# Two slack terms in a planned order, small passes on all partitions, and where the compressed scores run, in a two-layer hybrid decoder

## The chip, the cores and the metric

The kernel runs on one core of one Trainium2 chip. A core has four compute engines that each take their instructions in order: TensorE (PE in the profile), which multiplies matrices and transposes; VectorE (DVE); ScalarE (ACT); and GpSimd (POOL), which is all but unused here. SyncE (SP) issues the DMA transfers between the chip's main memory and the on-chip memory. The engines run side by side and wait for each other through semaphores only. PE's results land in PSUM, eight banks of 128 partitions by 512 float32 values; everything else lies in SBUF, also 128 partitions wide.

The metric is the device time of one execution in microseconds, the median of several runs.

## The reference

Two layers (`DEPTH` = 2) over a sequence of 256 positions with 1024 features. Each layer has two groups of attention heads side by side and a feed-forward part, each wrapped in RMS norms. All of it is float32.

```python
h = _rms_norm(x, g_pre_mix[l])
nq, kc, vc, ksel, vsel, kwin, vwin, gates, fq, fk, fv, ff = jnp.split(h @ w_in[l], split_at, axis=-1)
o_nsa = _nsa_mixer(...)        # 8 heads, 2 groups of keys and values
o_fox = _fox_mixer(...)        # 8 heads
mix = jnp.concatenate([o_nsa, o_fox], axis=-1) @ w_out[l]
x = x + _rms_norm(mix, g_post_mix[l])
h = _rms_norm(x, g_pre_mlp[l])
y = jnp.square(jax.nn.relu(h @ w_up[l])) @ w_down[l]
x = x + _rms_norm(y, g_post_mlp[l])
```

The sparse attention (`_nsa_mixer`) sums three branches under sigmoid gates. The compressed branch makes 15 blocks of 32 positions out of the keys and the values, sends each through a small network with a GELU (`gelu(blocks @ w1 + b1) @ w2 + b2`), and attends to the results:

```python
kc = _compress(k_c, pos_k, w1_k, b1_k, w2_k, b2_k)
vc = _compress(v_c, pos_v, w1_v, b1_v, w2_v, b2_v)
sc = jnp.einsum('bghqd,bgnd->bghqn', qp, kc) * scale
pc = _masked_softmax(sc, mc) * mc
o_cmp = jnp.einsum('bghqn,bgnd->bghqd', pc, vc)
```

The selected and the windowed branch attend to whole keys; at 256 positions both are plain causal attention with their own keys and values. The forgetting attention (`_fox_mixer`) adds differences of a running sum to its logits:

```python
log_f = jax.nn.log_sigmoid(f_logits + f_bias)
cum = jnp.cumsum(log_f, axis=1).transpose(0, 2, 1)
logits = einsum('bhqd,bhkd->bhqk', q, k) * scale + cum[:, :, q0:q1, None] - cum[:, :, None, :q1]
```

## The kernel before, in words

**Weights.** All weights come from main memory in pieces of 288 to 512 KB, in the order in which PE needs them (`Weights`, lines 465 to 500). A large float32 product is made of three products of half the width: each operand is split into `hi`, rounded to the type `fp32r`, and `lo`, the rounded rest; hi·hi, hi·lo and lo·hi are summed in PSUM (`mm3`, line 651). For a piece of weights ACT makes `whi` (a copy that rounds) and DVE makes `wlo` (a subtraction). The buffers are rings (`raw` of 9, `whi` and `wlo` of 7).

**Stages of a layer.** The input projection has six chunks of columns, c0 to c5. c0 and c1 hold the keys and values of the sparse part, the gates and the forget logits, c2 its queries, c3, c4 and c5 the queries (`fqT`), keys (`fkT`) and values (`fV`) of the forgetting part. The weights of the compressed branch's small network ride along with the pieces of c2 and c3 (`SEQ`, `RIDES`, `hidden_part`, line 884): at the fourth piece of c2 the 16 products for the keys run, at the fourth piece of c3 those for the values. They use only 32 columns of PE each, four of them side by side (`tile_position=(0, 32 * c)`; `kstk` and `kstv` are the stationary operands). Then follow, on other engines' help, `hidden_T` (line 899) and `hidden_gelu` (919) for the GELU, `compressed_k` (927), which leaves the keys as `kbd`, a block-diagonal tile for two heads, and `compressed_v` (937), which leaves the values split into halves in `vrep`; `compressed_vT` (953) transposes that into `vbig`. `compressed_scores` (964) is the four products `kbd` by `qT`, again on 32 columns each, `compressed_exp` (973), `compressed_scale` (985) and `compressed_T` (1001) are its softmax and transposes. `forget_sums` (1012) makes the running sum by a product with a triangle of ones and leaves `cum`: rounded values on partitions 0 to 31 and 64 to 95, the rounded rests on 32 to 63 and 96 to 127.

Attention itself goes over 24 entries of a list `flat` (line 1308): 16 for the sparse part (pair of heads, parity, branch) and 8 for the forgetting part ("fox"). For each there are scores (`nsa_scores` or `fox_scores`, in the score banks `s` and `x`), a masked maximum on DVE and an exponential on ACT (`pr`, with `st` for maxima and sums), the scaling by sum and gate on DVE (`scale`, line 1193), the transposes (`probs_T`, 1204: the products named `s<-cst,pr`), which ACT or DVE copies to `prT` or `prX`, and for each two pairs of heads a run of values' products (`pv`, 1222, in the bank `o`) on 64 columns each. `o_evac` (1240) splits the result into `oT` hi (ACT) and `oT` lo (DVE), which the output projection multiplies (the products `acc<-whi,oT` and so on). The `sandwich` (704) applies the norms; the MLP (lines 1392 to 1499) follows.

**Order.** Nothing is issued as it is written. A `Recorder` (line 171) records every operation with what it depends on. `stretch` (186) makes several PE products one unit; this is how the runs of small products stay together. `fill`, `fill_to` and `step` pull products of the projection's chunks between the steps of the attention, and a dictionary `side` (1310) names what else is called at which entry of `flat`; from there on an operation's key grows by `LANE` = 0.9 for each recorded operation. Each operation gets a planned cost in ns (`_cost`, 439, with `_latency` and `_product`). `schedule` (290) then plays all engines: at each moment each engine takes, of the operations that are ready and whose buffers fit, the one of lowest rank. For PE the rank is the key; for the others, from the second pass on, it is the time by which the operation must end so that PE's users in the pass before would not be late (`deadlines`, 247). A change of PE's tile size is charged with `ENTER` and `LEAVE` (line 367). `order` (275) makes one pass and `PASSES` = 4 further ones and keeps the one with the least planned end. `emit` (390) issues that order; so nearly all instructions stand at line 397 in the trace, and the names of tiles tell them apart. The planned times set the order only; on the chip each engine starts an instruction when its semaphores allow.

A load's planned end is when the bus is through with it, and 2900 ns (line 364).

Of the kernel before, what the change touches and what calls it, by code (L numbers as in the profile page):

```python
# [24 lines left out]
P = 128  # L25
# [11 lines left out]
LANDING = 2500.0  # L37
WAIT = 0.7
# [17 lines left out]
C_ID, C_ROPE, C_SID, C_TRI, C_MASK, C_CM, C_M01, C_SEL, C_END = np.cumsum(  # L56
    [0, 128, 64, 32, 256, 256, 32, 32, 16]).tolist()


def constants():  # L60
    c = np.zeros((P, C_END), np.float32)
    i = np.arange(P)
    c[:, C_ID:C_ID + P] = np.eye(P)
    causal = np.where(i[None, :] <= i[:, None], 0.0, NEG)
    c[:, C_MASK + 128:C_MASK + 256] = causal
    c[:, C_TRI:C_TRI + 128] = i[:, None] <= i[None, :]
    c[:, C_TRI + 128:C_TRI + 256] = 1.0
    inv = np.float32(500000.0) ** (-np.arange(8, dtype=np.float32) * np.float32(2.0) / np.float32(16.0))
    for t in range(NT):
        ang = (i + t * P).astype(np.float32)[:, None] * inv[None, :].astype(np.float32)  # L70
        o = C_ROPE + 32 * t
        c[:, o:o + 8] = c[:, o + 8:o + 16] = np.cos(ang)
        c[:, o + 16:o + 24] = -np.sin(ang)
        c[:, o + 24:o + 32] = np.sin(ang)
        ok = (16 * np.arange(16) + 31)[None, :] <= (i + t * P)[:, None]
        c[:, C_CM + 16 * t:C_CM + 16 * t + 16] = np.where(ok, 0.0, NEG)
        c[:, C_M01 + 16 * t:C_M01 + 16 * t + 16] = ok
    for h in range(8):
        c[h::32, C_SEL + h] = 1.0
    for m in range(32):  # L80
        c[m::32, C_SID + m] = 1.0
    return c
# [88 lines left out]
class Recorder:  # L171
# [21 lines left out]
    def add(self, engine, name, args, kw):  # L193
# [15 lines left out]
        op.cost = _cost(op, views)  # L209
# [80 lines left out]
    def schedule(self):  # L290
# [41 lines left out]
        while events:  # L332
# [5 lines left out]
            for e, ops in waiting.items():  # L338
                while busy[e] <= t:
# [21 lines left out]
                    if e == "sync":  # L361
                        busy[e] = t + 450
                        bus = max(bus, t + 1150) + best.cost
                        best.end = bus + 2900
                    else:
                        busy[e] = best.end = t + best.cost
                        if e == "tensor" and best.tile != tiled:
                            busy[e] = best.end = best.end + (tiled == (P, P)) * ENTER + (tiled != (P, P)) * LEAVE
                            tiled = best.tile
# [69 lines left out]
def _cost(op, views):  # L439

    out = op.args[0] if op.args else op.kw["out"]
    n = int(np.prod(out.shape[1:]))
    if op.engine == "sync":
        v = views[0][1]
        return v.shape[0] * int(np.prod(v.shape[1:])) * 4 / 360.0
# [5 lines left out]
    if op.engine == "vector":  # L451
# [7 lines left out]
        return 68 + 64 * aps + n * (0.52 if fast else 1.04) + 10 * (op.name == "tensor_tensor_reduce")  # L459
# [55 lines left out]
def trunk(nc, A, consts_in, out, sbp, pp):  # L515
    def tile(shape, dtype, name, tag=None, bufs=1):
        return nc.tile(sbp[(tag or name) not in OPERANDS], shape, dtype, name, tag, bufs)
# [108 lines left out]
    nc.vector.memset(kbd, 0.0)  # L626
    vrep = tile([P, 2, 4, 2, 16], F32R, name="vrep")
    nc.vector.memset(vrep.bitcast(F32), 0.0)
# [149 lines left out]
    for l in range(DEPTH):  # L778
# [105 lines left out]
        def hidden_part(s, q):  # L884
# [3 lines left out]
            if q == 3:  # L888
                T["hid"] = psum("o")
                with nc.stretch():  # L890
                    for i in range(16):
# [3 lines left out]
                                         start=i < 4, stop=i >= 12, tile_position=(0, 32 * c))  # L895
                T["hs" + s] = tile([P, 256], F32, name="hs", tag="cum")
# [29 lines left out]

        def compressed_k():
# [4 lines left out]
            for j in range(2):  # L932
                hh = slice(j * HD, j * HD + HD)
                nc.vector.tensor_scalar(kbd[hh, :, j, :], ps[hh, 0:32].rearrange("p (g n) -> p g n", g=2),
                                        par["smT"][hh, 36:37], None, op0=OP.add)

        def compressed_v():
# [3 lines left out]
            for c in range(2):  # L941
                nc.tensor.matmul(ps[:, 0:32], par["w2"]["v"][:, c].rearrange("p j d -> p (j d)"), T["ghv"][:, c, :],
                                 start=c == 0, stop=c == 1)
            vt = small([P, 2, 16], "vt", 1)
            nc.vector.tensor_scalar(vt, ps[:, 0:32].rearrange("p (g n) -> p g n", g=2), par["smT"][:, 37:38], None,
                                    op0=OP.add)
            for j in range(2):
                hh = slice(j * HD, j * HD + HD)
                x = vt[hh, :, None, :].to_broadcast([HD, 2, 2, 16])
                nc.vector.tensor_copy(vrep[hh, :, 0:2, j, :], x)  # L950
                nc.vector.tensor_sub(vrep[hh, :, 2:4, j, :], x, vrep[hh, :, 0:2, j, :].bitcast(F32))
# [12 lines left out]
        def compressed_scores():  # L964
            ps = psum("s")
            with nc.stretch():
              for p in range(4):
                nc.tensor.matmul(ps[32 * p:32 * p + 32, :S], kbd[:, p // 2].rearrange("p j n -> p (j n)"),
                                 T["qT"][:, p, :], start=True, stop=True, tile_position=(0, 32 * p))
            T["csT"] = small([P, S], "cs", 1)  # L970
            nc.scalar.activation(T["csT"], ps[:, :S], AF.Copy)

        def compressed_exp():
            ps = psum("s")
# [37 lines left out]
        def forget_sums():  # L1012
# [6 lines left out]
            cum = tile([P, 384], F32R, name="cum", tag="cum")  # L1019
            for o, n in ((0, P), (P, S)):  # L1020
                nc.scalar.activation(cum[:, o:o + n], ps[:, :n], AF.Copy)
            for r in (slice(32, 64), slice(96, 128)):
                for o, n in ((0, P), (P, S)):
                    nc.vector.tensor_sub(cum[r, o:o + n], ps[r, :n], cum[r, o:o + n].bitcast(F32))
# [277 lines left out]
        for t in range(NT):  # L1302
# [7 lines left out]
        side = {0: compressed_scores, 1: compressed_exp, 2: compressed_scale, 3: compressed_T,  # L1310
                4: lambda: (fill_to("c3"), hidden_T("v")), 5: lambda: hidden_gelu("v"),
# [236 lines left out]
```

## Time and profile before

| | |
|---|---|
| median of 3 runs | 627.24 us (627.1 to 627.25) |
| the profiled execution, its own time | 627.13 us |
| its span, from the first to the last instruction | 625.3 us |
| granted TensorE clock, mean | 0.998 |
| HBM traffic | 114.00 MB read, 1.05 MB written, 184 GB/s over the span |
| largest group of instructions on DVE | `wlo`, 188 passes, 225.4 us |
| largest group on ACT | `whi`, 188 passes, 195.2 us |
| largest group on PE | `s<-xT,whi`, 448 products of 512 columns, 112.0 us |

How to read it: the profile is one execution, taken by the hardware profiler. The span is what the trace covers; the 1.8 us between it and the execution's own time lie outside the trace. An instruction's line in a view gives the line of the kernel (here that of `emit`), the engine, the operation, the tile written and the tiles read, their sizes, and a count where equal neighbours are drawn together. PE's products are pipelined: their busy times overlap, so that the distance between two starts, not the busy time, is what a product costs. "PEld" is PE's loading of stationary operands, which overlaps with products. A name in brackets behind an instruction, such as [0.19 <-DVE vrep L397], is the time for which the engine waited ahead of it and what ended the wait.

In the page's 40 slices of the span PE is at nine tenths or more in all but the last. DVE is at eight or nine tenths from 16 to 125 us and again from 313 to 406 us, the attention of the two layers, and mostly at five to seven in the MLPs.

### The profile page before, as it was taken

How to read it: one execution, taken by the hardware profiler on the slowest of the kernel's cores; microseconds unless marked ns; L12 is line 12 of the kernel's file. 1: busy time of each engine (PE TensorE's matmuls, PEld its weight loads, DVE VectorE, ACT ScalarE, POOL GpSimd, SP SyncE). 2: the span in 40 equal slices, each digit the busy share in tenths (PEclk: the TensorE clock that was granted, in tenths of full speed). 3: DMA queues.
4: the chain of work that ended last, by engine and by line, in shares of the span. 5: the costliest groups of instructions: out<-in, count | busy, mean ns of one | idle time of the engine just before them, and what ended most of it. 6: DMA issues, size and time to landing. Idle time of an engine off the chain costs nothing.

```text
span 625.3 us, 9919 instructions
## 1 busy us (share of the span) xinstructions
PE 616.8 (99%) x3572; PEld 517.7 (83%) x3572; DVE 477.9 (76%) x1053; ACT 375.8 (60%) x728; POOL 0.2 (0%) x4
## 2 busy tenths in 40 slices
PE   9999999999999999999999999999999999999995
PEld 7988977788888888888888988777888888888884
DVE  6889998879966566567698899976996666566544
ACT  7768776567655455555476766764766555455432
POOL 0000000000000000000000000000000000000000
PEclk9999999999999999999999999999999999999999
DMA  8988555319666666654348682622386556666001
GB/s 324 404 310 285 199 161 157 91 64 320 221 200 202 187 183 203 193 178 128 117 129 273 231 313 67 226 85 95 123 306 187 191 179 198 197 179 202 24 1 67
DMA packets 33600, 115.69 MB, mean 185 GB/s; under 512 B 3984, under 2 KB 4112, under 8 KB 33552
## 3 DMA queue, kind: packets, MB, share of 16 engines
q1 hardware_dynamic: 33552, 115.07, 56.5%
q8 instruction: 28, 0.46, 0.3%
q14 instruction: 20, 0.16, 0.1%
HBM read 114.00 MB, written 1.05 MB: 184 GB/s over the span
## 4 chain that ended last, share of the span: by engine, by line
PE 87%; DVE 10%; issue 1%; DMA 1%; ACT 0%; DVEq 0%; SPq 0%
PE s L397 33%; PE acc L397 25%; PE x L397 24%; PE o L397 6%; DVE wlo L397 3%; DVE pr L397 3%; DMA first<-in_first_dram 1%; DVE gz L397 1%; DVE cs L397 0%; DVE fqT L397 0%; DVE prT L397 0%; DVE st L397 0%; DVE prX L397 0%; ACT whi L397 0%; DVE vrep L397 0%
## 5 line engine op out<-in xcount | busy, mean ns | idle before, releaser
L397 DVE TENSOR_TENSOR wlo<-wraw,whi 128x1024 fp32r<-128x1024 f32 (+1 forms) x188 | 225.4, 1203 | 85.1 <-ACT whi L397 81.9
L397 ACT ACTIVATE whi<-wraw 128x1024 fp32r<-128x1024 f32 (+1 forms) x188 | 195.2, 1042 | 111.8 <-PE acc L397 64.6
L397 PE MATMUL s<-xT,whi 128*128 128x512 f32 x448 | 112.0, 392 | 0.0
L397 PEld LDWEIGHTS s<-xT,whi 128*128 128x128 f32 x448 | 81.4, 189 | 15.2
L397 PE MATMUL acc<-whi,aT 128*128 128x512 f32 x256 | 88.6, 390 | 0.0
L397 PE MATMUL x<-whi,aT 128*128 128x512 f32 x256 | 88.4, 390 | 0.0
L397 PEld LDWEIGHTS s<-xT,wlo 128*128 128x128 f32 x448 | 61.1, 190 | 4.4
L397 PE MATMUL s<-xT,wlo 128*128 128x256 f32 x448 | 62.5, 282 | 0.0
L397 ACT ACTIVATE pr<-pr,st 128x256 f32<-128x256 f32 (+1 forms) x96 | 43.2, 452 | 24.8 <-DVE st L397 21.9
L397 PEld LDWEIGHTS acc<-whi,aT 128*128 128x128 f32 x256 | 48.1, 188 | 9.9
L397 PEld LDWEIGHTS x<-whi,aT 128*128 128x128 f32 x256 | 48.1, 188 | 9.7
L397 PE MATMUL acc<-wlo,aT 128*128 128x512 f32 x128 | 50.0, 390 | 0.0
L397 PE MATMUL x<-wlo,aT 128*128 128x512 f32 x128 | 50.0, 390 | 0.0
L397 PE MATMUL acc<-xT,whi 128*128 128x256 f32 x256 | 49.8, 286 | 0.0
L397 PEld LDWEIGHTS acc<-xT,whi 128*128 128x128 f32 x256 | 40.6, 190 | 1.6 <-ACT whi L397 0.4
L397 ACT ACTIVATE rl<-h 128x512 f32<-128x512 f32 x28 | 17.7, 633 | 35.8 <-DVE h L397 35.8
L397 PE MATMUL x<-whi,xT 128*128 128x512 f32 x112 | 37.1, 403 | 0.1
L397 PE MATMUL acc<-xT,wlo 128*128 128x256 f32 x128 | 36.4, 284 | 0.0
L397 PE MATMUL acc<-whi,xT 128*128 128x512 f32 (+1 forms) x128 | 36.3, 356 | 0.0
L397 DVE TENSOR_TENSOR h<-rl 128x512 f32<-128x512 f32 x28 | 19.4, 692 | 16.8 <-ACT rl L397 16.8
L397 ACT ACTIVATE rl<-x 128x512 f32<-128x512 f32 x24 | 14.8, 617 | 24.5 <-PE x L397 18.7
L397 PEld LDWEIGHTS acc<-wlo,aT 128*128 128x128 f32 x128 | 24.0, 188 | 4.9
(222 smaller groups left out, 975.4 us busy)
## 6 DMA issues: line engine op xcount, KB each, us to landing
wraw<-in_w_up_dram SPq DMA_DIRECT2D x64, 512.0 KB, 3.7
wraw<-in_w_down_dram SPq DMA_DIRECT2D x64, 512.0 KB, 3.5
wraw<-in_w_in_dram SPq DMA_DIRECT2D x36, 512.0 KB, 4.9
wraw<-in_w_out_dram SPq DMA_DIRECT2D x16, 512.0 KB, 5.6
w<-in_cmp_w_k_dram SPq DMA_DIRECT2D x8, 512.0 KB, 6.0
w<-in_cmp_w_v_dram SPq DMA_DIRECT2D x8, 512.0 KB, 5.8
first<-in_first_dram SPq DMA_DIRECT2D x7, 384.0 KB, 6.0
wraw<-in_w_in_dram SPq DMA_DIRECT2D x8, 288.0 KB, 4.3
```

Of the source, the lines that this page charges most:

```text
L397: getattr(getattr(self.nc, op.engine), name)(*[real(v) for v in args], **{k: real(v) for k, v in kw.items()})
```

## The change

Four things are changed.

The planner's costs: each DVE and ACT operation costs 20 ns more in the plan (`SLACK`), and a DVE operation that writes fewer than 128 partitions 100 ns more (`part`). A load's landing is the same 2900 ns, written as 900 + `LATE`.

Passes on parts of the partitions become passes on all: `kbd` and the compressed values `vt` are now made by `by_half`, for each group of keys one pass over all 128 partitions that multiplies by a constant which is one on the half of the partitions that belongs to the head and zero on the other (`C_HALF`). With the zeros written each time, the two memsets at the kernel's start go. `vrep` hi is one pass on ACT and `vrep` lo one on DVE, in place of two and two passes on DVE over 64 partitions each. `forget_sums` has two ACT copies into a new tile `two` (its ring is that of `rl`): `hi`, and the sum times `C_REST`, which is one on the partitions of the rests and zero elsewhere; two passes on DVE over all partitions then form `cum`, in place of two ACT copies and four DVE subtractions on 32 partitions each.

The compressed scores: the four products `kbd` by `qT` stand in the stretch of the values' 16 products in `hidden_part`, behind them; their copy out of PSUM is the first step of `compressed_exp`.

The places of the steps: `side` now calls `fill_to("c3")` at entry 0 (which brings the values' products with it), `compressed_exp` at 1, `compressed_scale` and `hidden_T("v")` at 2, `compressed_T` and `hidden_gelu("v")` at 3; `compressed_v` at 6 and all behind it stay.

```diff
+SLACK, LATE = {"vector": 20, "scalar": 20}, 2000
...
-C_ID, C_ROPE, C_SID, C_TRI, C_MASK, C_CM, C_M01, C_SEL, C_END = np.cumsum(
-    [0, 128, 64, 32, 256, 256, 32, 32, 16]).tolist()
+C_ID, C_ROPE, C_SID, C_TRI, C_MASK, C_CM, C_M01, C_SEL, C_HALF, C_REST, C_END = np.cumsum(
+    [0, 128, 64, 32, 256, 256, 32, 32, 8, 2, 2]).tolist()
...
+    for j in range(2):
+        c[j * HD:j * HD + HD, C_HALF + j] = 1.0
+
+    c[:, C_REST] = i // 32 % 2
+    c[:, C_REST + 1] = 1 - i // 32 % 2 * 2
...
-        op.cost = _cost(op, views)
+        op.cost = _cost(op, views) + SLACK.get(engine, 0)
...
-                        best.end = bus + 2900
+                        best.end = bus + 900 + LATE
...
+    part = 100 * (out.shape[0] < P)
...
-        return 68 + 64 * aps + n * (0.52 if fast else 1.04) + 10 * (op.name == "tensor_tensor_reduce")
+        return 68 + part + 64 * aps + n * (0.52 if fast else 1.04) + 10 * (op.name == "tensor_tensor_reduce")
...
-    nc.vector.memset(kbd, 0.0)
...
-    nc.vector.memset(vrep.bitcast(F32), 0.0)
...
+                    if s == "v":
+                        compressed_scores()
...
+        def by_half(dst, ps, bias):
+
+            for g in range(2):
+                nc.vector.scalar_tensor_tensor(dst[:, g], ps[:, None, 16 * g:16 * g + 16].to_broadcast([P, 2, 16]),
+                                               par["smT"][:, bias:bias + 1],
+                                               cst[:, C_HALF:C_HALF + 2, None].to_broadcast([P, 2, 16]), op0=OP.add, op1=OP.mult)
+
...
-            for j in range(2):
-                hh = slice(j * HD, j * HD + HD)
-                nc.vector.tensor_scalar(kbd[hh, :, j, :], ps[hh, 0:32].rearrange("p (g n) -> p g n", g=2),
-                                        par["smT"][hh, 36:37], None, op0=OP.add)
+            by_half(kbd, ps, 36)
...
-            vt = small([P, 2, 16], "vt", 1)
-            nc.vector.tensor_scalar(vt, ps[:, 0:32].rearrange("p (g n) -> p g n", g=2), par["smT"][:, 37:38], None,
-                                    op0=OP.add)
-            for j in range(2):
-                hh = slice(j * HD, j * HD + HD)
-                x = vt[hh, :, None, :].to_broadcast([HD, 2, 2, 16])
-                nc.vector.tensor_copy(vrep[hh, :, 0:2, j, :], x)
-                nc.vector.tensor_sub(vrep[hh, :, 2:4, j, :], x, vrep[hh, :, 0:2, j, :].bitcast(F32))
+            vt = small([P, 2, 2, 16], "vt", 1)
+            by_half(vt, ps, 37)
+            x = vt.rearrange("p g j n -> p g (j n)")[:, :, None, :].to_broadcast([P, 2, 2, 32])
+            hi, lo = (vrep[:, :, b:b + 2].rearrange("p g a j n -> p g a (j n)") for b in (0, 2))
+            nc.scalar.activation(hi, x, AF.Copy)
+            nc.vector.tensor_sub(lo, x, hi.bitcast(F32))
...
-            ps = psum("s")
-            with nc.stretch():
-              for p in range(4):
+            T["cps"] = ps = psum("s")
+            for p in range(4):
                 nc.tensor.matmul(ps[32 * p:32 * p + 32, :S], kbd[:, p // 2].rearrange("p j n -> p (j n)"),
                                  T["qT"][:, p, :], start=True, stop=True, tile_position=(0, 32 * p))
+
+        def compressed_exp():
             T["csT"] = small([P, S], "cs", 1)
-            nc.scalar.activation(T["csT"], ps[:, :S], AF.Copy)
-
-        def compressed_exp():
+            nc.scalar.activation(T["csT"], T["cps"][:, :S], AF.Copy)
...
+            two = tile([P, 2, S], F32R, name="two", tag="rl", bufs=2)
+            hi, rest = two[:, 0], two[:, 1].bitcast(F32)
+            nc.scalar.activation(hi, ps[:, :S], AF.Copy)
+            nc.scalar.activation(rest, ps[:, :S], AF.Copy, scale=cst[:, C_REST:C_REST + 1])
             for o, n in ((0, P), (P, S)):
-                nc.scalar.activation(cum[:, o:o + n], ps[:, :n], AF.Copy)
-            for r in (slice(32, 64), slice(96, 128)):
-                for o, n in ((0, P), (P, S)):
-                    nc.vector.tensor_sub(cum[r, o:o + n], ps[r, :n], cum[r, o:o + n].bitcast(F32))
+                nc.vector.scalar_tensor_tensor(cum[:, o:o + n], hi[:, :n].bitcast(F32), cst[:, C_REST + 1:C_REST + 2],
+                                               rest[:, :n], op0=OP.mult, op1=OP.add)
...
-        side = {0: compressed_scores, 1: compressed_exp, 2: compressed_scale, 3: compressed_T,
-                4: lambda: (fill_to("c3"), hidden_T("v")), 5: lambda: hidden_gelu("v"),
+        side = {0: lambda: fill_to("c3"), 1: compressed_exp, 2: lambda: (compressed_scale(), hidden_T("v")),
+                3: lambda: (compressed_T(), hidden_gelu("v")),
                 6: compressed_v, 7: compressed_vT, 8: forget_sums, 14: lambda: fill_to("c4"), 17: lambda: fill_to("c5")}
```

The program has as many PE products after the change as before. The order on all engines is made anew by the planner; the prediction goes by the two orders as they come out of it.

## The prediction

> **What bounds the kernel now.** I read the page first, then the busy time by stage, then the chain of work that ended last, then TensorE's (PE) timeline at the places that the change touches.
>
> ```profile
> span 625.3 us, 9919 instructions
> PE 616.8 (99%) x3572; PEld 517.7 (83%) x3572; DVE 477.9 (76%) x1053; ACT 375.8 (60%) x728; POOL 0.2 (0%) x4
> PE 87%; DVE 10%; issue 1%; DMA 1%; ACT 0%; DVEq 0%; SPq 0%
> ```
>
> PE is busy 616.8 of 625.3 us, so hardly a gap can be closed. But a busy PE may still be a late one, and 10% of the chain lies on VectorE (DVE). The stages tell where (columns: stretch, its length, then busy us and count of PE, PE's weight loads, DVE, ACT, POOL; clock, DMA share, GB/s):
>
> ```profile
> 60.00:76.00 16.00, 15.81 (x129) 15.20 (x128) 15.85 (x65) 11.58 (x31) 0.00 (x0) 1.00 0.69 248
> 92.00:112.00 20.00, 20.00 (x137) 14.54 (x136) 17.96 (x63) 13.88 (x39) 0.00 (x0) 1.00 0.53 157
> 145.00:300.00 155.00, 155.00 (x791) 132.49 (x790) 107.74 (x131) 86.44 (x123) 0.00 (x0) 1.00 0.64 201
> ```
>
> In the sparse attention of a layer (60 to 76 us) PE and DVE are both full. In the later part (92 to 112) DVE has 2.0 us free of 20. In the MLP (145 to 300) PE is alone. The chain between 44 and 80 us (start, us, what):
>
> ```profile
> 48.16 1.23 DVE wlo L397
> ...
> 57.18 0.60 DVE fqT L397
> ...
> 69.40 0.32 DVE pr L397
> ...
> 70.99 1.12 DVE wlo L397
> ...
> 72.81 0.57 DVE prX L397
> ...
> 73.65 0.23 DVE vrep L397
> ...
> 74.02 0.93 PE s L397 x7
> ```
>
> From 48 to 74 us the chain runs along DVE and is handed to PE at `vrep`; from there to the end it stays on PE. So two things can be gained: PE work itself, and the few moments at which PE is late behind DVE. Both are small.
>
> **The change, part by part.** Sums are made against the profiled execution's 627.13 us: 625.3 of span and 1.8 around it; the median of the runs is 0.1 higher.
>
> *1. The compressed scores join the run of small tiles.* Both ways of running `tile_position=(0, 32 * c)` products stand in the trace, alone:
>
> ```profile
> 35.75 0.39 PE L397 MATMUL x<-whi,xT 128*128 128x512 f32 x1
> 36.07 1.93 PE L397 MATMUL o<-w,kstk 128*32 128x256 f32 x32
> 37.94 0.50 PE L397 MATMUL acc<-xT,whi 128*128 128x256 f32 x2
> 38.27 0.28 PE L397 MATMUL acc<-xT,wlo 128*128 128x256 f32 x1
> ...
> 53.12 0.39 PE L397 MATMUL x<-kx,qS 128*128 128x512 f32 x1
> 53.45 0.64 PE L397 MATMUL s<-qT,kbd 128*32 128x256 f32 x8
> 54.02 0.50 PE L397 MATMUL acc<-xT,whi 128*128 128x256 f32 x2
> 54.36 0.28 PE L397 MATMUL acc<-xT,wlo 128*128 128x256 f32 x1
> ```
> ```profile
> 613.35 5.45 PE acc L397 x24
> ```
>
> A plain product of 512 columns takes 5.45/24 = 0.23 us from start to start, one of 256 columns 0.12. The first run therefore occupies PE from 35.75 + 0.23 = 35.98 to 37.94, and the pair behind it takes 0.33 instead of 0.24: 2.05 us for 32 passes. The scores: 53.35 to 54.02, and 0.10 behind: 0.77 for 8 passes. Four groups of 8 and one group differ by 1.28, so a group is 0.43 and what a visit costs besides is 0.34. The scores keep their group and lose the visit, once a layer: 2 x 0.34 = **0.68 us less**. No row shows two different products in one run; if the visit's cost stays, the gain is 0. I take the whole, since the row of 32 shows four groups with other weights in one visit.
>
> [...]
>
> What the run now waits for: its last four products need `kbd`, and `kbd` stands in DVE's queue behind both `fqT` passes; all of PE is queued behind it. In layer 0, from the last product of c3's first half on, PE has 16 products of 256 columns, one of 512 and four groups of the run ahead: 16 x 0.12 + 0.23 + 4 x 0.43 = 3.9 us. DVE needs 2 x 0.60 and two small passes (part 3, 0.25 each), 1.7, and 0.1 to 0.2 for the handoff at either end: about 2.0. That leaves 1.9 us of cover, more than one `wlo` pass of 1.12. Cost: nothing; with the cover gone, what DVE is late, up to 1 us a layer.
>
> *2. The order.* The cost of every DVE and ACT instruction is raised by 20, of those on part of the partitions by 100 more, so the planner puts PE's users of their results later. PE's work is the same: 3,344 matmuls in both; the 859 of the first MLP and the last 871 stand in the same order. In the attention PE's visits to smaller tiles fall from 22 to 18: two by part 1, two because fox scores and the values' products now follow each other directly. That saves between 0 and a whole visit each; I take half of 0.34, as each place has three changes of mode instead of four: 2 x 0.17 = **0.34 less**.
>
> Where PE is late now (what precedes in the rows is the start, the busy time, the count):
>
> ```profile
> 73.43 0.40 PE L397 MATMUL acc<-xT,whi 128*128 128x256 f32 x2
> 74.02 0.33 PE L397 MATMUL s<-identr,vrep 128*128 128x128 f32 x2 [0.19 <-DVE vrep L397]
> ...
> 83.37 1.29 PE L397 MATMUL s<-cst,pr 128*128 128x128 f32 x6
> ```
> ```profile
> 380.98 0.28 PE L397 MATMUL acc<-xT,whi 128*128 128x256 f32 x1
> 381.43 0.34 PE L397 MATMUL s<-identr,vrep 128*128 128x128 f32 x2 [0.16 <-DVE vrep L397]
> ...
> 389.67 0.87 PE L397 MATMUL s<-cst,pr 128*128 128x128 f32 x6
> ...
> 391.32 0.39 PE L397 MATMUL acc<-wlo,xT 128*128 128x512 f32 x1
> 392.04 0.50 PE L397 MATMUL s<-kx,qS 128*128 128x256 f32 x2 [0.34 <-DVE st L397]
> ```
>
> At `vrep` PE is 0.59 - 0.24 = 0.35 late in layer 0 and 0.45 - 0.12 = 0.33 in layer 1. In the new order 14 products of 512 columns (9 `whi`, 5 `wlo`) stand ahead of the first `vrep` transposes that stood behind before: 14 x 0.23 = 3.2 us more cover; 9 in layer 1, 2.0 us. DVE's queue ahead of the same point gains one `wlo` (1.12) and two `fkT` (as `fqT`, 0.60 each), loses one `prX` (0.57) and one pair of `pr` scalings (0.32 and a bit less): 1.2 more. So 2.0 and 0.8 us of lead are won, against 0.35 and 0.33 of lateness. I take both waits as gone: **0.68 less** (bounds 0 and 0.68).
>
> The six `pr` transposes at 83.37 take 0.42 longer than the same six at 389.67; at 391.32 PE stands 0.72 - 0.23 = 0.49. With these two and some three smaller ones of 0.1 to 0.2 I count 1.3 us of other lateness. Summed over both orders in such durations, PE's 48 rounds of `pr` transposes come later against DVE's scalings in 39 cases, by up to 7 us, and earlier in 9, by at most 1.6; there the trace has at least 1.8 us between scaling and transposes. So the old waits should mostly go; but the order is new everywhere, and I take half: **0.66 less** (bounds 0 and 1.3).
>
> What gets tighter is the way out of the values' products:
>
> ```profile
> 119.68 0.50 PE L397 MATMUL acc<-whi,oT 128*128 128x512 f32 x1
> ```
> ```profile
> 119.80 0.60 ACT L397 ACTIVATE oT<-o 128x512 fp32r<-128x512 f32 x1 [1.83 <-PE o L397]
> ```
> ```profile
> 120.43 0.69 DVE L397 TENSOR_TENSOR oT<-o,oT 128x512 fp32r<-128x512 f32 x1 [0.43 <-ACT oT L397]
> ```
>
> From 119.68, PE's first product after the run, `oT`'s upper part is ready at 120.40 (0.72) and its lower part at 121.12 (1.44). Before, 12 products stand between the last fox run and the first that needs its `oT`; now 4 (0.9 us), and 7 for the lower part (1.6). Behind the second sparse run there were 19, now six transposes alone (0.63 to 0.67 by 389.67 and its like) in layer 0 and three products more in layer 1. By the rows this is just enough for fox and 0.05 to 0.2 short for the sparse one. At the start, the loads of `x` and the chains of `rsqrt` for both row blocks now go ahead of the third piece of c1's weights; I allow 0.2 for it. New waits in all: **0.4 more** (bounds 0 and 1.7, four handoffs each a bit late).
>
> *3. All partitions.* Off PE's path; it thins DVE's queue:
>
> ```profile
> L397 DVE TENSOR_SCALAR kbd<-s,w 64x32 f32<-64x32 f32 x4 | 1.0, 247 | 0.0
> L397 DVE TENSOR_TENSOR vrep<-vt,vrep 64x64 fp32r<-64x64 f32 x4 | 0.9, 220 | 0.1
> L397 DVE CAST vrep<-vt 64x64 fp32r<-64x64 f32 x4 | 0.8, 191 | 0.1
> ...
> L397 DVE TENSOR_TENSOR cum<-s,cum x8: 283/356/429, 78.7 to 386.3; 32x256 fp32r<-32x256 f32 x4, 32x128 fp32r<-32x128 f32 x4
> ...
> L397 DVE SCALAR_TENSOR_TENSOR z<-acc,rsqrt,bias 128x32 f32<-128x32 f32 x4 | 1.0, 243 | 0.0
> L397 DVE SCALAR_TENSOR_TENSOR xT<-first,gcol,xT 128x256 fp32r<-128x256 f32 x7 | 3.4, 483 | 0.0
> ```
>
> A layer now spends 2 x 0.247 + 2 x 0.220 + 2 x 0.191 + 4 x 0.356 = 2.74 us on these. After: `kbd` and one `vt` more as `z`, 3 x 0.243; one `vrep` pass of 128 columns, at most 0.29; `cum` twice, as `xT` 0.48 and at most that again less a third: 1.9 in all. ACT takes one pass of 128 columns and a wider `cum` one, beside 40% of idle time. DVE gains some 0.9 us a layer, already within part 2's waits; alone it is worth 0 on PE's path. The two memsets that go lie in the first 2 us, before DVE's first data arrive: 0.
>
> **Sum.** 627.13 - 0.68 - 0.34 - 0.68 - 0.66 + 0.4 = 625.17; on the runs' median 0.1 more: **625.3 us**.
>
> **The rivals.** *A: only PE's own work changes.* DVE is full from 48 to 74 us in any order; then the waits change places and are not fewer, and 0.68 + 0.34 are left: 626.2 us, no change that can be told. For it: DVE's 15.85 of 16 us. Against it: the lead at nearly all handoffs grows, and the chain has DVE on it up to 74 us only.
>
> *B: the thin cover behind the values' products decides; slower.* ACT or DVE may have begun a pass over weights when a run ends:
>
> ```profile
> L397 ACT ACTIVATE whi<-wraw 128x1024 fp32r<-128x1024 f32 (+1 forms) x188 | 195.2, 1042 | 111.8 <-PE acc L397 64.6
> ```
>
> Then `oT` comes up to 1.04 later by ACT, and 1.12 by a `wlo` ahead on DVE; PE had 2.7 us of cover for this, now 0.67 to 0.9. At two runs a layer, 4 x 1.1 = 4.4 more, against the 2.4 gained by parts 1 and 2: 627.2 + 2.0 = 629.2 us. It decides from 0.2 us of ACT's or DVE's lateness on. Against it: in the new queues ACT has a `prT` copy or an exponential just ahead of these `oT`, and DVE's two `wlo` ahead of the last one have nearly 5 us of PE's work (13 products, three transposes and the run itself) to finish in.
>
> **How the numbers follow.** Forecast 0.62, A 0.25, B 0.13. About 0.2% (1.25 us) can be told from no change: below 626.0 is faster, above 628.5 slower. Low end: both successions whole, all waits gone, no new one: 627.23 - 0.68 - 0.68 - 0.68 - 1.3 = 623.9. High end: part 1's 0.68 alone and 1.3 of new waits: 627.8. Faster 0.62, same 0.25, slower 0.13.
>
> **What would show it.** The scores' 8 passes stand behind the 32 of `kstv`, 0.43 us longer in all, with no visit of their own; the `vrep` transposes start without a wait in both layers; the products at the end of each run of values' products show waits below 0.2 us; the MLP stages keep 155.0 us. Wrong, if PE shows waits of 0.5 us or more for `oT`, `kbd` or the score banks.

## The result and the profile after

The changed kernel takes 622.94 us in the median of six runs (622.81 to 623.51), the kernel before 627.24 us beside it: a ratio of 0.9932, 95% interval 0.992 to 0.9945. That is 4.3 us faster; 1.9 us were predicted, and the time lies below the range's low end of 623.9 us. The profiled execution took 622.97 us, about 1.9 of them outside its span.

The page of the changed kernel, its first lines and its chain:

```profile
span 621.0 us, 9923 instructions
PE 613.3 (99%) x3572; PEld 518.0 (83%) x3572; DVE 476.3 (77%) x1043; ACT 376.3 (61%) x730; POOL 0.2 (0%) x4
PE 99%; DVE 0%; issue 0%; DVEq 0%; ACT 0%
```

The chain that ended last no longer runs along DVE between 48 and 74 us; it is PE's own work from the first product to the last. PE executes as many products as before; its busy time is 3.5 us less for them. That is more than the changes of tile size can account for (1.4 us, below), so the view had shown a part of the waits as busy time.

The same three stretches as before (columns as in the prediction):

```profile
60.00:76.00 16.00, 16.00 (x123) 15.14 (x122) 14.80 (x60) 11.76 (x34) 0.00 (x0) 1.00 0.72 272
92.00:112.00 20.00, 20.00 (x141) 15.01 (x139) 18.97 (x75) 14.97 (x47) 0.00 (x0) 1.00 0.54 187
145.00:300.00 155.00, 155.00 (x791) 132.48 (x790) 106.91 (x131) 85.77 (x122) 0.00 (x0) 1.00 0.60 201
```

From 60 to 76 us DVE now has 1.2 us free where it had 0.15; from 92 to 112 us it is 1.0 us fuller, and PE has a single wait there, of 0.14 us (below). The MLP is the same. Over the whole kernel DVE is busy 1.6 us less, so what PE gained was not bought by much less work on DVE.

PE's timeline of the changed kernel around the values' run with the scores, and at `vrep` in both layers:

```profile
54.62 1.93 PE L404 MATMUL o<-w,kstv 128*32 128x256 f32 x32
56.37 0.61 PE L404 MATMUL s<-qT,kbd 128*32 128x256 f32 x8
56.91 0.38 PE L404 MATMUL acc<-xT,wlo 128*128 128x256 f32 x1
...
76.27 0.40 PE L404 MATMUL acc<-wlo,xT 128*128 128x512 f32 x1
76.50 0.29 PE L404 MATMUL s<-identr,vrep 128*128 128x128 f32 x2
...
380.52 0.40 PE L404 MATMUL acc<-whi,xT 128*128 128x512 f32 x1
380.76 0.28 PE L404 MATMUL s<-identr,vrep 128*128 128x128 f32 x2
```

The run of 40 passes takes 56.91 - 54.62 = 2.29 us; the run of 32 passes in the prediction took 37.94 - 36.07 = 1.87. The scores cost 0.42 us, as foretold (0.43). The products ahead of `vrep` take 0.23 and 0.24 us to the next start, the bare price of 512 columns: both waits are gone.

**A count of PE's waits.** To compare kernels, I took for each PE product the distance from its start to the next start, and subtracted what a product of its kind between the same kinds of neighbours takes undisturbed (the value that a fifth of them stay below, over all 19 traces of this case). What is left above 0.04 us, from 10 us on, is summed as "waits". In the first 10 us PE waits for the first data; those waits vary from execution to execution between 0.66 and 1.36 us and are kept apart. "Rest" is the span less both: the work, with its changes of tile size. "Visits" are the changes from whole-array products to smaller tiles.

| kernel | median us | visits | waits us | rest us |
|---|---|---|---|---|
| before | 627.24 | 22 | 3.08 | 621.5 |
| changed | 622.94 | 18 | 0.14 | 620.1 |

So 2.94 us came from waits and 1.37 us from the rest. The waits of before are many: `vrep` 0.35 and 0.32, the two large ones of the prediction 0.42 and 0.61, and a dozen more of 0.05 to 0.3 us at the handoffs to `q_rot`, `pcs`, `lf`, `kW` and the score banks. One of the dozen, in the kernel before:

```profile
336.25 0.40 PE L397 MATMUL x<-whi,xT 128*128 128x512 f32 x1
336.59 0.52 PE L397 MATMUL s<-cst,kW 128*128 128x128 f32 x3
```

The product of 512 columns takes 0.34 us to the next start where 0.23 is the undisturbed price, and no bracket names the 0.11 us.

**What the four visits were worth.** They are not alike. A visit of the scores, merged into another run of the same tile size, saves 0.34 us, as above, twice. The other two are fox scores (64x128 tiles) that now stand directly ahead of values' products (128x64 tiles). Before:

```profile
98.22 0.40 PE L397 MATMUL o<-pcT,vbig 128*128 128x512 f32 x1
98.54 0.93 PE L397 MATMUL s<-fkT,fqT 64*128 64x128 f32 x8
...
99.58 0.50 PE L397 MATMUL x<-wlo,oT 128*128 128x512 f32 x1
99.91 0.49 PE L397 MATMUL s<-cst,pr 128*128 128x128 f32 x3
100.33 0.87 PE L397 MATMUL o<-prT,vS 128*64 128x256 f32 x8
...
103.08 0.50 PE L397 MATMUL x<-whi,oT 128*128 128x512 f32 x1
```

and after:

```profile
101.28 0.93 PE L404 MATMUL s<-fkT,fqT 64*128 64x128 f32 x8
...
102.31 0.87 PE L404 MATMUL o<-prT,vS 128*64 128x256 f32 x8
...
105.06 0.88 PE L404 MATMUL s<-cst,pr 128*128 128x128 f32 x6
```

Apart, the two runs take 99.58 - 98.54 = 1.04 and 103.08 - 100.33 = 2.75 us; together they take 105.06 - 101.28 = 3.78, so nothing is saved inside. What goes is one way into small tiles and one way out: 98.54 - 98.22 = 0.32 instead of 0.23 ahead of a run, and 99.91 - 99.58 = 0.33 instead of 0.23 behind it. That is 0.2 us for each of these two. About 0.3 us of the 1.37 remain. Most of it is what stands behind the runs: ten of the 18 runs are now followed by transposes, six of the 22 before, and by the starts in the traces the way out then costs 0.06 us (0.165 to the next start behind the first transpose, where 0.109 is undisturbed) and not 0.11 (0.338 behind a product of 512 columns, where 0.231 is).

### The profile page after: what moved, and what is told of

It is laid out like the page before. It is cut to its first block, busy times and chain, and to the rows that moved or that the text cites. A ratio compares the mean times of both kernels' runs of the same rounds, so it can differ in the third digit from the quotient of the medians.

```text
span 621.0 us, 9923 instructions
## 1 busy us (share of the span) xinstructions
PE 613.3 (99%) x3572; PEld 518.0 (83%) x3572; DVE 476.3 (77%) x1043; ACT 376.3 (61%) x730; POOL 0.2 (0%) x4
## 4 chain that ended last, share of the span: by engine, by line
PE 99%; DVE 0%; issue 0%; DVEq 0%; ACT 0%
PE s L404 35%; PE acc L404 31%; PE x L404 25%; PE o L404 7%; DVE x L404 0%; DVE m L404 0%; DVEq L1555 0%; DVE rsqrt L404 0%; DVE warm L404 0%; ACT rl L404 0%; DVEq L404 0%
## 5 line engine op out<-in xcount | busy, mean ns | idle before, releaser
L404 PE MATMUL acc<-whi,xT 128*128 128x512 f32 (+1 forms) x128 | 38.8, 361 | 0.0
L404 PEld LDWEIGHTS x<-wlo,aT 128*128 128x128 f32 x128 | 24.1, 188 | 4.5
```

The costliest lines, as they stand in the source:

```text
L404: getattr(getattr(self.nc, op.engine), name)(*[real(v) for v in args], **{k: real(v) for k, v in kw.items()})
```

## The experiments

All are compared with the kernel before, run on the same chip. The table gathers them; the reading follows.

| run | what it is | median us | visits | waits us | rest us |
|---|---|---|---|---|---|
| e1 | before, scores merged | 625.43 | 17 | 1.88 | 620.4 |
| e2 | before, all planner costs | 623.53 | 19 | 0.33 | 620.5 |
| e3 | before, passes on all partitions | 624.50 | 22 | 0.38 | 621.4 |
| e4 | changed, no planner costs | 623.97 | 18 | 0.57 | 620.2 |
| e5 | before, 100 ns for partial passes | 625.37 | 22 | 1.03 | 621.5 |
| e6 | before, 20 ns for all | 625.53 | 20 | 1.98 | 620.9 |
| e7 | before, LANE 0.91 | 626.91 | 22 | 2.80 | 621.4 |
| e8 | before, LANE 0.89 | 627.23 | 21 | 3.04 | 621.4 |
| e9 | changed, scores apart | 624.08 | 21 | 0.41 | 620.9 |
| e10 | changed, old passes | 623.27 | 17 | 0.28 | 620.1 |
| e11 | changed, -20 ns for all | 628.10 | 18 | 4.84 | 620.8 |
| e12 | changed, 40 ns for all | 626.33 | 17 | 3.40 | 620.3 |
| e13 | changed, LANE 0.91 | 623.10 | 17 | 0.24 | 620.0 |
| e14 | changed, 10 ns for all | 623.04 | 17 | 0.14 | 620.1 |
| e15 | changed, 25 ns for all | 622.99 | 16 | 0.14 | 620.1 |
| e16 | changed, no 100 ns | 623.10 | 17 | 0.14 | 620.0 |
| e17 | changed, one product between | 623.96 | 19 | 1.04 | 620.9 |

### The change in three parts: e1 to e4

e1 is the kernel before with the scores and the dictionary `side` of the change:

```diff
+                    if s == "v":
+                        compressed_scores()
...
-            ps = psum("s")
-            with nc.stretch():
-              for p in range(4):
+            T["cps"] = ps = psum("s")
+            for p in range(4):
...
-        side = {0: compressed_scores, 1: compressed_exp, 2: compressed_scale, 3: compressed_T,
+        side = {0: lambda: fill_to("c3"), 1: compressed_exp, 2: lambda: (compressed_scale(), hidden_T("v")),
```

> The kernel before with the compressed scores moved into the values' run and the new places of the steps, nothing else; planner costs and passes as before. Main theory (the waits of PE go because the plan leaves DVE and ACT slack): only PE's changes of tile size are saved, about 1.2 us, and the waits stay: 626.0 us. Rival (the new places of the steps take the waits away, slack or not): 623.2 to 624.0 us.

Measured: 625.43 us, ratio 0.9966 (0.9953 to 0.9978). The 1.1 us of rest are there, and 1.2 us of waits went too; 1.9 remain. Neither theory had the size: the scores and the places of the steps remove some of the waits, not most.

e2 is the kernel before with the plan's costs alone:

```diff
+SLACK, LATE = {"vector": 20, "scalar": 20}, 2000
...
-        op.cost = _cost(op, views)
+        op.cost = _cost(op, views) + SLACK.get(engine, 0)
...
+    part = 100 * (out.shape[0] < P)
```

> The kernel before with the planner's costs alone (20 ns on each DVE and ACT operation, 100 ns on DVE operations of fewer than 128 partitions); the scores keep a visit of their own. Main theory: about 3.0 us of waits go and some 0.5 us of changes of tile size, 623.7 us. Rival (the places of the steps): 626.5 to 627.2 us.

Measured: 623.53 us, ratio 0.9938 (0.9926 to 0.9951), as the main theory said. Costs that exist only in the plan, with every instruction as before, bring 3.9 of the 4.3 us.

e3 is the changed kernel without the plan's costs and without the scores' new place, so that the passes over all partitions are left:

```diff
-        op.cost = _cost(op, views) + SLACK.get(engine, 0)
+        op.cost = _cost(op, views)
...
-    part = 100 * (out.shape[0] < P)
...
-                    if s == "v":
-                        compressed_scores()
```

> The kernel before with the passes over all partitions alone. Main theory: DVE's 0.9 us a layer do not reach PE by themselves, 627.2 us within 0.5. Rival (a thinner DVE queue is what takes the waits away): 1.5 us less or more than that, 625.7 us or below.

Measured: 624.50 us, ratio 0.9953 (0.9941 to 0.9966): the main theory fell here, and the time lies where the rival had it. All visits stayed, and the waits went from 3.08 to 0.38 us with no slack in the plan.

e4 is the changed kernel without `SLACK` and `part`.

```diff
-        op.cost = _cost(op, views) + SLACK.get(engine, 0)
+        op.cost = _cost(op, views)
...
-    part = 100 * (out.shape[0] < P)
```

> The changed kernel without the planner's costs: scores in the values' run, steps in their new places, passes over all partitions. Main theory: the waits come back, 3.0 us, and the tile changes stay saved: 625.9 us. Rival (the places of the steps): as the changed kernel, 623 us.

Measured: 623.97 us, ratio 0.9945 (0.9932 to 0.9959). It has 0.57 us of waits, not 3, so the main theory fell here too; the rival's 623 was not quite reached. Without the slack too, the passes and the scores' place remove most of the waits.

So two parts of the change, the plan's costs and the passes, remove nearly all of the same waits, each by itself. What they have in common is seen in DVE's timeline of the kernel before at the passes on 64 and 32 partitions:

```profile
52.55 0.51 DVE L397 TENSOR_SCALAR kbd<-s,w 64x32 f32<-64x32 f32 x2
53.09 0.29 DVE L397 CUSTOM_DVE_ANT_0 pr<-s,cst 128x128 f32<-128x128 f32 x1
...
72.00 0.28 DVE L397 TENSOR_SCALAR vt<-s,w 128x32 f32<-128x32 f32 x1
72.16 0.31 DVE L397 CUSTOM_DVE_ANT_0 pr<-s,cst 128x128 f32<-128x128 f32 x1
...
73.40 0.47 DVE L397 TENSOR_TENSOR vrep<-vt,vrep 64x64 fp32r<-64x64 f32 x2
73.90 0.43 DVE L397 CUSTOM_DVE_ANT_0 pr<-x,cst 128x256 f32<-128x256 f32 x1
...
78.69 1.47 DVE L397 TENSOR_TENSOR cum<-s,cum 32x256 fp32r<-32x256 f32 x4
80.17 0.56 DVE L397 COPY prX<-s 128x384 f32<-128x384 f32 x1
```

and of the changed kernel:

```profile
53.47 0.40 DVE L404 SCALAR_TENSOR_TENSOR kbd<-s,w,cst 128x32 f32<-128x32 f32 x2
53.78 0.28 DVE L404 CUSTOM_DVE_ANT_0 pr<-s,cst 128x128 f32<-128x128 f32 x1
```

Two `kbd` passes on 64 partitions hold DVE for 53.09 - 52.55 = 0.54 us, 0.27 each: the first lasts 0.236 us and the second starts 0.251 us after the first's start, when it is through. On 128 partitions they take 0.31, 0.16 each: the first lasts 0.244 us and the second starts 0.158 us after the first's start, before it has ended. The operations differ, but the operation that made `kbd` before, when it writes `vt` on 128 partitions, is followed after 72.16 - 72.00 = 0.16 us as well. By the formula at line 459 the plan of before gives such a pass 68 + 64 + 32 x 1.04 = 165 ns. It is right for the pass on all partitions and 0.1 us short for the partial one. For two `vrep` subtractions it has 2 x 135 = 269 ns, DVE took 0.50 us; for the four of `cum` 1070 ns, DVE took 1.48 us. With two `kbd`, four `vrep` and four `cum` passes a layer, the plan is about a microsecond short in all, at three places where DVE is full, and PE's products had been placed by the plan. Some 2.3 of the 3.08 us of waits lie from 73 to 86 us and from 381 to 393 us, at and behind the `vrep` and `cum` passes of the two layers. The `part` term tells the plan; with the passes over all partitions the old plan comes true. That this is why e3 is faster is argued: its passes also take 0.9 us a layer off DVE (the prediction's estimate), and no run gives DVE that relief while the plan stays short.

### Which of the plan's costs, or any other order: e5 to e8

e5 has only `part`, e6 only `SLACK`, e7 and e8 only another `LANE`, in the kernel before (of e5 and e6 one line each):

```diff
+    part = 100 * (out.shape[0] < P)
```
```diff
-        op.cost = _cost(op, views)
+        op.cost = _cost(op, views) + SLACK.get(engine, 0)
```
```diff
-LANE = 0.9
+LANE = 0.91
```
```diff
-LANE = 0.9
+LANE = 0.89
```

> The kernel before, the plan's DVE operations on fewer than 128 partitions 100 ns dearer, no other slack. Theory P (the plan of before takes 80 to 95 ns too little for each of these passes, 13 a layer, and PE's waits come from that): about 2.3 us of waits go, 624.9 us. Theory S (the 20 ns on every operation do it): 626.7 to 627.4 us. Theory D (the order of before is one of many of about equal plans and happened to be a poor one, any other is better): about 625 us too, so e7 and e8 must tell D from P.

> The kernel before, 20 ns more on each DVE and ACT operation in the plan, nothing for partial passes. PE makes 20 visits to smaller tiles instead of 22, two of the runs directly behind another. Theory P: the visits and little else, 626.4 us. Theory S: 2.6 us of waits and 0.4 us of visits, 624.2 us. Theory D: about 625 us.

> The kernel before with LANE = 0.91 in place of 0.9, a change that gives no engine more time and no operation another cost; the order changes in about 500 lines of PE's listing, the visits stay 22. Theories P and S: 627.2 us within 0.6, since the plan is as tight as before. Theory D: about 625 us.

> The kernel before with LANE = 0.89; 21 visits, one run directly behind another. Theories P and S: 627.0 us within 0.6. Theory D: about 625 us.

Measured: e5 625.37 us, ratio 0.997 (0.9957 to 0.9982); e6 625.53 us, 0.9972 (0.9962 to 0.9982); e7 626.91 us, 0.9993 (0.9984 to 1.0002); e8 627.23 us, 1.0 (0.9991 to 1.0009). Theory D fell: two other orders with the old costs have 2.8 and 3.0 us of waits, at the same places. The 100 ns alone take 2.0 us of waits away, with the partial passes still there; so for two thirds of them it is enough that the plan knows. The 20 ns alone take 1.1 us, and two visits. P had e5 half a microsecond too low and e6 0.9 too high, so both costs work, and together (e2) they add up: 1.9 and 1.8 against 3.9 us.

The largest wait that 20 ns everywhere leave open is again next to partial passes. PE's timeline of e6:

```profile
73.78 0.28 PE L399 MATMUL acc<-xT,wlo 128*128 128x256 f32 x1
74.77 0.50 PE L399 MATMUL acc<-whi,xT 128*128 128x512 f32 x1 [0.71 <-DVE fkT L399]
```

and DVE's:

```profile
73.00 0.41 DVE L399 CAST vrep<-vt 64x64 fp32r<-64x64 f32 x2
73.44 0.56 DVE L399 COPY prX<-s 128x384 f32<-128x384 f32 x1
74.03 1.29 DVE L399 TENSOR_TENSOR fkT<-acc,rT 128x512 f32<-128x512 f32 x2
```

PE's next product goes into the `acc` bank that `fkT` empties, and `fkT` stands behind `vrep` and `prX` on DVE: 0.87 us, the largest single wait of that kernel. The two casts hold DVE for 73.44 - 73.00 = 0.44 us where the plan, with its 20 ns, has 0.24; what makes the rest of the 0.87 was not taken apart.

### What each part is worth inside the change: e9, e10, e16

e9 takes the scores' new place and `side` out of the changed kernel (e1's edit reversed), e10 puts the old passes back and keeps `part`, e16 leaves `part` out. The first lines of each edit:

```diff
-                    if s == "v":
-                        compressed_scores()
```
```diff
-            by_half(kbd, ps, 36)
+            for j in range(2):
+                hh = slice(j * HD, j * HD + HD)
+                nc.vector.tensor_scalar(kbd[hh, :, j, :], ps[hh, 0:32].rearrange("p (g n) -> p g n", g=2),
+                                        par["smT"][hh, 36:37], None, op0=OP.add)
```
```diff
-    part = 100 * (out.shape[0] < P)
```

> The changed kernel with the compressed scores in a visit of their own and the steps in their old places; planner costs and passes as changed. 21 visits to smaller tiles (18 in the changed kernel). If the merged run is worth the visits it saves: 3 visits of about 0.3, 623.8 us. If its place also takes waits away that the slack does not: 624.5 us or more. If it is worth nothing: 622.9 us.

> The changed kernel with the passes on 32 and 64 partitions of before, at the plan's 100 ns more for each. 17 visits. If only the plan's knowledge of these passes counts and not DVE's time in them: 622.9 us, within 0.5. If DVE's time counts (0.9 us a layer): 623.9 us or more.

> The changed kernel without the 100 ns for partial passes, of which only those that gather the blocks are left; 17 visits. If these 100 ns no longer matter once the passes are on all partitions: 622.9 us within 0.4. If they do: 623.5 us or more.

Measured: e9 624.08 us, ratio 0.9948 (0.9935 to 0.996): three visits more, 0.8 us of rest, and 0.27 us of waits. e10 623.27 us, 0.9937 (0.9924 to 0.9949), within the 0.5 of the first alternative: with the plan told, the passes over all partitions are worth 0.3 us. e16 623.10 us, 0.9934 (0.9922 to 0.9947): with only the gathering of the blocks left as partial passes, telling the plan of them is worth nothing that can be told from no change.

### How much slack: e11 to e15

In the changed kernel, `SLACK` of -20 and 40 ns, likewise 10 and 25, and `LANE` 0.91 with the 20 ns kept:

```diff
-SLACK, LATE = {"vector": 20, "scalar": 20}, 2000
+SLACK, LATE = {"vector": -20, "scalar": -20}, 2000
```
```diff
-SLACK, LATE = {"vector": 20, "scalar": 20}, 2000
+SLACK, LATE = {"vector": 40, "scalar": 40}, 2000
```
```diff
-LANE = 0.9
+LANE = 0.91
```

> The changed kernel with each DVE and ACT operation 20 ns cheaper in the plan instead of 20 dearer; 18 visits as in the changed kernel. If PE's waits follow the time that the plan gives these engines: more waits than without slack (624.0 us), 624.8 to 626 us. If slack works only by a chance of the order: 622.9 to 624 us.

> The changed kernel with 40 ns on each DVE and ACT operation; 17 visits. The trace of the changed kernel has about 0.2 us of waits of PE left in the attention, so no more than that and one visit can be gained: 622.4 to 622.9 us. If too much slack makes PE change tiles or wait for buffers more often: 623.2 us or more.

> The changed kernel with LANE = 0.91, which gives no engine more time; the order changes in some 870 lines of PE's listing, 17 visits. If the slack gives lead at nearly all handoffs: 622.9 us within 0.6. If the changed kernel's order is a lucky one among those with slack: 623.6 to 626 us.

> The changed kernel with 10 ns in place of 20, 17 visits. If the time follows the slack up to 20: between 624.0 (no slack) and 622.9, about 623.4 us. If each order is a draw: anywhere from 622.5 to 626.5 us.

> The changed kernel with 25 ns in place of 20, 16 visits, two more runs directly behind another than in the changed kernel. If 40 ns is where new waits begin and 25 is as good as 20: 622.5 us, the two visits saved. If new waits grow with the slack from 20 on: 623.5 to 624 us.

Measured: e11 628.1 us, ratio 1.0012 (1.0003 to 1.0021), slower than the kernel before and beyond the first alternative's 624.8 to 626 us, with 4.8 us of waits in 39 places; e12 626.33 us, 0.9985 (0.9976 to 0.9994); e13 623.1, e14 623.04 and e15 622.99 us, all with ratios of 0.993 and intervals of some 0.0013 to either side. So from 10 to 25 ns, and in another order with the same slack, the time is the same: the changed kernel's order is no lucky one. The two visits that e15 saves, again fox scores directly ahead of values' products, bring nothing that can be told, where 0.4 us were expected. Less than none is worse still, and 40 ns is 3.4 us slower than 20, far more than the second alternative had in mind. There the waits are at new places. ACT's timeline of e12:

```profile
128.85 2.01 ACT L404 ACTIVATE whi<-wraw 128x1024 fp32r<-128x1024 f32 x2
130.76 0.58 ACT L404 ACTIVATE rl<-acc 128x512 f32<-128x512 f32 x1
...
131.33 0.58 ACT L404 ACTIVATE xT<-s 128x512 fp32r<-128x512 f32 x1
...
412.99 0.51 ACT L404 ACTIVATE pr<-pr,st 128x256 f32<-128x256 f32 x1 [1.40 <-DVE st L404]
...
413.50 0.39 ACT L404 ACTIVATE pr<-pr,st 128x128 f32<-128x128 f32 x1
...
413.88 0.57 ACT L404 ACTIVATE oT<-o 128x512 fp32r<-128x512 f32 x1
```

and PE's:

```profile
130.18 1.53 PE L404 MATMUL s<-cst,mg 128*128 128x128 f32 x8
131.97 0.50 PE L404 MATMUL s<-whi,xT 128*128 128x512 f32 x1 [0.25 <-ACT xT L404]
...
413.20 0.87 PE L404 MATMUL s<-cst,pr 128*128 128x128 f32 x6
414.51 0.50 PE L404 MATMUL x<-whi,oT 128*128 128x512 f32 x1 [0.44 <-ACT oT L404]
```

At 413 us an exponential stands ahead of `oT` on ACT, and PE has six transposes for cover: 0.68 us late. In the sandwich at 129 to 133 us two `whi` passes, then a square, stand ahead of `xT`: 1.4 us in all. Why the plan with 40 ns puts them there was not settled.

### A visit by itself: e17

```diff
             T["cps"] = ps = psum("s")
+            nc.tensor.matmul(ps[:, S:S + P], ident_r, ident_r, start=True, stop=True)
             for p in range(4):
```

> The changed kernel with one whole-array product of 128 columns (the identity by itself, into unused columns of the scores' bank) between the values' 16 products and the 4 of the scores, so that these make a visit of their own again; 19 visits. If a visit costs 0.34 us wherever it stands: 0.34 and about 0.08 for the product, twice, 623.8 us, and in PE's timeline the stretch from the last projection product before the run to the first two behind it 0.42 us longer. If the saving came from the scores' place and not from the visit: 0.08 twice, 623.1 us.

PE's timeline of e17:

```profile
55.76 1.93 PE L404 MATMUL o<-w,kstv 128*32 128x256 f32 x32
57.62 0.33 PE L404 MATMUL s<-identr 128*128 128x128 f32 x1
57.88 0.64 PE L404 MATMUL s<-qT,kbd 128*32 128x256 f32 x8
58.45 0.39 PE L404 MATMUL acc<-xT,wlo 128*128 128x256 f32 x1
```

The run takes 58.45 - 55.76 = 2.69 us, 0.40 more than the changed kernel's 2.29 (0.42 expected), and 0.40 in layer 1 as well. In both layers a whole visit was paid again with one product of the other tile size between. The median, 623.96 us (623.58 to 624.78), ratio 0.9946 (0.9932 to 0.9959), is 1.0 us above the changed kernel, where 0.8 were expected; the profiled execution is the slowest of the five, with a wait of 0.8 us for weights at 33 us that the changed kernel does not have.

No kernel tried here beats the changed one by more than runs differ; 622.94 to 623.10 us is reached by five.

## Why the prediction was off, point by point

**Direction and forecast.** Faster was right, and each of the terms in the sum had the right sign. Rival A fell: the waits did not change places. Rival B's mechanism did not decide here, but its like exists: in e12, at 413 us, `oT` is 0.68 us late, behind an exponential and not behind a pass over weights. All that the prediction named under "What would show it" came out, and none of it measured the term that failed.

**Part 1, the merged scores: right.** 0.68 us predicted; the run grew by 0.42 us where a visit of their own cost 0.77, 0.7 us for both layers, and e17 shows the price by itself. `kbd` was ready in time: its passes end at 53.87 us, and PE reaches the scores at 56.37 us.

**Fox scores directly before values' products: right, nearly.** I took half a visit for each of two places (three changes of mode, that is of PE's tile size, instead of four), 0.34 us; the timelines show 0.2 for each, 0.4 us. The rest fell by some 0.3 us more than both kinds of visits explain. That comes mostly from transposes directly behind the runs, which the prediction did not count.

**`vrep`: right.** 0.68 us of waits, both gone.

**Other lateness: the step that failed.** "With these two and some three smaller ones of 0.1 to 0.2 I count 1.3 us of other lateness" - there were 2.4 us of it (3.08 less the 0.67 at `vrep`). I had looked at the waits that a bracket names and at two large gaps; a dozen waits of 0.05 to 0.3 us without a bracket were counted as three. And "I take half" was wrong as well: nearly all went; one wait of 0.14 us is left. I had the comparison of 39 rounds with more lead and 9 with less in hand, and did not follow it to its end. By this step alone the sum was 1.8 us too high.

**New waits: 0.4 us taken, 0.14 found.** The one there is stands where it was foreseen, behind the second sparse run of layer 0, where six transposes were counted as 0.05 to 0.2 us short:

```profile
105.06 0.88 PE L404 MATMUL s<-cst,pr 128*128 128x128 f32 x6
105.83 0.50 PE L404 MATMUL x<-whi,oT 128*128 128x512 f32 x1
```

From 105.06 to 105.83 are 0.77 us, where six transposes alone take 0.63. In layer 1, with three products more, there is none. The 0.2 us for the start was not needed: the waits of the first 10 us are 0.77 us in this execution, 0.76 before.

**All partitions.** "Alone it is worth 0 on PE's path" was wrong: e3 is 2.9 us faster than the kernel before. I priced DVE's time in these passes, 0.9 us a layer, but not that the plan before had them too short, so that an order made by it was late behind them (e5, which changes the plan's knowledge alone, takes 2.0 us of waits away). The rows that I quoted, 247 ns for `kbd` beside the formula's 165, would have shown it. Inside the whole change, where the costs already tell the plan, my 0 comes close: 0.3 us (e10).

**The sum.** 2.94 us of waits instead of 0.94 and 1.37 us of rest instead of the 1.02 of the visits make up the 2.3 us between forecast and result. The range's low end took all waits as gone, but of the 1.98 us that I had counted.

## What to carry to other kernels

Where an engine is full and follows an order that was planned, its lateness is worth counting product by product (start to start, against the same product undisturbed) before a gain is bounded: many small waits add up to more than the few that a view names. Compare the plan's durations with the trace's, start to start, for each kind of pass; a kind that is 0.1 us too short in the plan can make PE late behind it. Telling the plan of it brought 1.9 us here (e5), the faster passes by themselves 2.9 (e3), and once the plan was told and had its slack, the faster passes brought 0.3 more (e10). Runs of the same tile size were worth putting together (0.34 us each here); runs of two tile sizes in a row gained less (0.2 us). A little slack on the helpers' costs (10 to 25 ns here) is robust, but more of it is not better, and it has to be measured.

## What the runs showed of the hardware that was not expected

The two `kbd` passes of the kernel before, 32 columns on 64 partitions each, one on either half, take 0.1 us more of DVE's time apiece than the two of the changed kernel, with as many columns on 128 partitions (0.27 against 0.16 us from start to start), though the mean duration of a pass is nearly the same, 247 and 244 ns. Whether the number of partitions or the place where they begin makes the difference, no run separates. And in e17, with a single product of 128 columns between two runs of small tiles, the way out and back in cost about as much as the visit that the scores had for themselves: 0.40 us with that product, where 0.34 and about 0.08 were expected. Two runs of different small tile sizes directly behind one another (64x128 and 128x64) saved 0.2 us against two visits, two of the same tile size 0.34 us.
